# Third FFN: 16 of its 22 hidden units by seven block products in place of eight

## The chip, the cores and the metric

The kernel runs on one core of a Trainium2 chip. The metric is the device time of one execution in microseconds (us). Before the change, three runs took 1701.3, 1697.54 and 1699.22 us: a median of 1699.22. Times below are from these runs or from one profiled execution of the kernel.

## The reference

Two streams of 256 tokens each, 1024 wide in float32 ("latent" and "context"), go through two layers. Each layer has a half-step feed-forward network (FFN), a mixer (attention in the first layer, a gated recurrence in the second), and a second FFN. Scale, shift and gate of each step come from a conditioning vector times a large matrix ("modulation"). The FFN reads:

```python
def half_ffn(h, shift, scale, gate, w_in, w_out, g, b):
    xm = modulate(h, shift, scale)
    a, u = jnp.split(xm @ w_in, 2, axis=-1)
    y = (jax.nn.silu(a) * u) @ w_out
    return post_norm(h, 0.5 * gate * y, g, b)
```

`w_in` is 1024 x 5632 and `w_out` 2816 x 1024. The change concerns the third of the four FFNs, the first of layer 1, which treats both streams (512 tokens).

## The kernel before

**Layout.** Activations lie with the 1024 features in 8 blocks of 128 partitions and the 512 tokens along the free axis: 0 to 255 latent (`LAT`), 256 to 511 context (`CTX`). `xh` and `xl` hold the FFN's modulated input, `h` the residual.

**Precision.** Every float32 operand is split in two parts: ScalarE casts it to a reduced float32 type (`h`, line 194), and VectorE subtracts to get the rest (`l`, line 199, helper `split`). `mm3` (lines 211, 214, 215) makes three matmuls per block: high by high, high by low, low by high. A weight block is 128 x 128.

**One FFN** (`ffn`). The hidden width 2816 is 22 units of 128. `unit_in` for unit j multiplies its `a` and `u` columns (8 blocks each, 3 passes: 48 matmuls) with 512 tokens; `ffn_g` then forms silu(a) * u (lines 521, 522) and splits it into `gh`, `gl`. The units go in two parts of 11. After each part, `unit_out` makes the 8 output blocks: 11 hidden blocks of 3 passes each, accumulated in one PSUM bank, then added to `h` through the gate (line 557). In the first part the four lead units (`LEAD`) run on the latent tokens first and on the context tokens later, as 256-wide matmuls, since the context's norm is still being finished (`LEADSTEP`). In the second part the last four output blocks (`TAIL`) are also made in halves, the latent half first, so that the next norm (`norm`, stepped by `TAILSTEP`) starts while matmuls continue.

**Weights.** A chunk is 128 x 1024 floats (512 KB), loaded by the SyncE queue (`raw`, line 179) into one of `RAW = 3` buffers and split into one of `WB = 7` pairs. A unit needs two chunks, an output block 1.375. `Stream` fetches chunks as they are asked for; `Keep` keeps them for a second use.

**Modulation rows.** `ada` loads one row of the modulation matrix (512 KB, two buffers) and VectorE takes its product with the conditioning vector (line 290). The third FFN carries 32 such rows; `side` spreads them as two after each unit and each output block, in the order written.

**Order of work.** The program is written with tiles. At compile time a planner puts the instructions of each engine in a fixed order: by the order in the program, but an instruction whose inputs or buffers are not ready in the planner's own timing can be overtaken by later ones. Instructions marked with `pin` keep their order among themselves. Tiles of one tag share a fixed number of buffers; here: `raw` 3, `w` 7, `tmp` 6, and 6 PSUM banks for `mm` and 2 for `ps`.

Of the kernel before, what the change touches and what calls it, by code (L numbers as in the profile page):

```python
# [33 lines left out]
SH = 16  # L34
# [2 lines left out]
RMS_EPS = 1e-6  # L37
HEADS = 8
MH = 4
QK_SCALE = 128.0 ** -0.5  # L40
BIG = 1.0e30

RAW = 3
WB = 7

NSTART = 4
# [4 lines left out]
TAIL = 4  # L51
# [90 lines left out]
class Body:  # L142
# [382 lines left out]
    def ffn(self, layer, s, gate, groups, side, start=None):  # L525
        nc, V = self.nc, self.nc.vector
        li = layer * 2 + s
        allg = BOTH
        call = lambda *k: side.get(k, lambda: None)()
        with self.tc.tile_pool(name=f"ffn{li}", bufs=1) as gp:  # L530
            self.gp, self.gt, self.gw, self.gn = gp, {}, T, NFH
            done = 0
            if start:
                start(self)
                done = NSTART

            def unit_in(j, w, g, steps={}):
                n = g[1] - g[0]
                pa, pu = self.mm(), self.mm()
                for k in range(ND):  # L540
                    for part, o in ((0, pa), (1, pu)):
                        self.mm3(o[:, :n], w(k * 2 + part), self.x(k, g), k == 0, k == ND - 1)
                    self.steps(steps.get((j, k), ""))
                self.ffn_g(j, pa, pu, g)

            def unit_out(hf, d, w, g, steps={}):
                t0, t1 = g
                y = self.mm()
                for i in range(NFH):
                    gh, gl = self.gt[hf * NFH + i]  # L550
                    self.mm3(y[:, : t1 - t0], w(d * NFH + i), (gh[:, t0:t1], gl[:, t0:t1]), i == 0, i == NFH - 1)
                    self.steps(steps.get((int(g == CTX), d - (ND - TAIL), i), ""))
                for gg in groups:
                    if gg[0] >= t0 and gg[1] <= t1:
                        v = 0 if gg[0] == 0 else 1
                        z = self.h[:, d, gg[0] : gg[1]]
                        V.scalar_tensor_tensor(z, y[:, gg[0] - t0 : gg[1] - t0], gate()[:, v, d : d + 1], z, ALU.mult, ALU.add)  # L557
                        if hf:
# [4 lines left out]
            for hf in range(2):  # L563
                js = list(range(hf * NFH, (hf + 1) * NFH))[0 if hf else done :]
                if hf == 0 and not start:
                    first = js[:LEAD]
                    ws = {j: Keep(self, [w_in[2 * j + i] for i in range(2)], SH) for j in first}
                    for g in groups:
                        assert len(self.running) == (g == LAT)
                        for j in first:  # L570
                            unit_in(j, ws[j], g, LEADSTEP if g == LAT else {})
                    for j in first:
# [11 lines left out]
                w = Stream(self, [w_out[hf * NFH + i] for i in range(NFH)])  # L584
                body = ND - TAIL if hf else ND
                for d in range(body):
                    unit_out(hf, d, w, allg)
                    call("out", hf, d)
                if body < ND:
                    w = Keep(self, w.chunks, SH, w)  # L590
                    self.fine = True
                    for g in groups:
                        for d in range(body, ND):
                            unit_out(hf, d, w, g, TAILSTEP)
                    self.steps(ENDSTEP)


    def ffn_last(self, layer, gate):
        nc, V, S, a = self.nc, self.nc.vector, self.nc.scalar, self.a
# [662 lines left out]
def emit(ctx, tc, a, out):  # L1262
    b = Body(ctx, tc, a, out)
    nc, V, S = b.nc, b.nc.vector, b.nc.scalar
# [4 lines left out]
    queue = [  # L1269
        [(0, p, both2) for p in range(16, 72)],  # L1270
        [(1, p, both2) for p in range(40)],
        [(1, p, (0,)) for p in range(40, 72)],
    ]
    made = {}

    def once(key, f):
        def get():
            if key not in made:
                made[key] = f()
            return made[key]  # L1280
        return get

    def side(key, coef, keep=(True, True), nxt=True, ada=(), alone=False):
        def pop():
            for _ in range(3 if len(ada) > 40 else 2):
# [6 lines left out]
        s = {}  # L1292
        for j in range(NF):
# [14 lines left out]
    b.ffn(1, 0, once("g2", lambda: b.half_gate(1, 2)), both, side("n3", lambda: b.ln_mod(1, 0, (1, 3)), (True, False), ada=queue[2]))  # L1308
# [9 lines left out]
def _layout(inputs):  # L1318
    f = lambda n: np.asarray(inputs[n])
# [7 lines left out]
    A["ada_w"] = f("ada_w").transpose(0, 2, 1).reshape(2, 72, P, D)  # L1327
    w = f("ffn_w_in").reshape(4, ND, P, 2, NF, P).transpose(0, 4, 2, 1, 3, 5)
    w_in = w.reshape(4, NF, P, 2, 1024).transpose(0, 1, 3, 2, 4).reshape(4, 2 * NF, P, 1024).copy()
    A["ffn_in"] = w_in  # L1330
    A["start_in"] = w[0, :NSTART].transpose(2, 1, 0, 3, 4).reshape(ND, P, 1024)
    w = f("ffn_w_out").reshape(4, 2, NFH, P, ND, P).transpose(0, 1, 4, 2, 3, 5)
    A["ffn_out"] = w.reshape(4, 2 * NFH, 8, P, P).transpose(0, 1, 3, 2, 4).reshape(4, 2 * NFH, P, 1024)
    A["ffn_last"] = f("ffn_w_out")[1, 1].reshape(NF, P, D)
    A["ln_row"] = np.stack([f("ln_g")[1, 2], f("ln_b")[1, 2]]).reshape(2, 4, TL)
# [12 lines left out]
    w = f("att_w_in")[0]  # L1348
# [50 lines left out]
```

## Time and profile before

| | |
|---|---|
| median of three runs | 1699.22 us (1697.54 to 1701.3) |
| span of the profiled execution | 1693.6 us |
| TensorE (PE) busy | 1643.8 us, 97% |
| VectorE (DVE) busy | 1231.7 us, 73% |
| ScalarE (ACT) busy | 656.3 us, 39% |
| GpSimd (POOL) busy | 93.6 us, 6% |
| read from memory | 247.83 MB |

The span runs from the first to the last instruction that the profiler saw; the page gives no other time for that execution, and 1699.22 is 5.6 us more. The page names instructions by engine, line and shape: "128x512 f32 x93 | 54.0, 585" are 93 instructions, 54.0 us busy together, 585 ns each on average. After a second bar stands the engine's idle time before them and what ended it. Matmuls overlap in the pipeline, so a matmul's duration is longer than the distance to the next.

### The profile page before, as it was taken

How to read it: one execution, taken by the hardware profiler on the slowest of the kernel's cores; microseconds unless marked ns; L12 is line 12 of the kernel's file. 1: busy time of each engine (PE TensorE's matmuls, PEld its weight loads, DVE VectorE, ACT ScalarE, POOL GpSimd, SP SyncE). 2: the span in 40 equal slices, each digit the busy share in tenths (PEclk: the TensorE clock that was granted, in tenths of full speed). 3: DMA queues.
4: the chain of work that ended last, by engine and by line, in shares of the span. 5: the costliest groups of instructions: out<-in, count | busy, mean ns of one | idle time of the engine just before them, and what ended most of it. 6: DMA issues, size and time to landing. Idle time of an engine off the chain costs nothing.

```text
span 1693.6 us, 24765 instructions
## 1 busy us (share of the span) xinstructions
PE 1643.8 (97%) x9432; PEld 1441.6 (85%) x9432; DVE 1231.7 (73%) x2681; ACT 656.3 (39%) x1125; POOL 93.6 (6%) x114
## 2 busy tenths in 40 slices
PE   7999999999899999999999999999999999999997
PEld 6888888899887898888888998888889878999986
DVE  6799977659988899996334977643335967998687
ACT  5622133215465452212331543213322645556541
POOL 0000000002321100000000100000001001120000
PEclk9999999999999999999999999999999999999999
DMA  9576765412102346774222257642221232337542
GB/s 356 184 230 231 236 210 199 149 62 77 61 2 82 119 136 234 229 244 152 93 94 75 101 179 247 215 144 98 99 100 63 94 125 76 113 125 246 178 168 94
DMA packets 71910, 250.49 MB, mean 148 GB/s; under 512 B 7920, under 2 KB 10480, under 8 KB 71792
## 3 DMA queue, kind: packets, MB, share of 16 engines
q1 hardware_dynamic: 71072, 248.15, 43.1%
q8 instruction: 74, 1.21, 0.3%
q10 hardware_dynamic: 720, 0.76, 0.1%
q14 instruction: 44, 0.36, 0.1%
HBM read 247.83 MB, written 1.05 MB: 147 GB/s over the span
## 4 chain that ended last, share of the span: by engine, by line
PE 83%; DVE 11%; ACT 3%; DMA 2%; issue 1%; POOL 0%; ACTq 0%; DVEq 0%; SPq 0%
PE t L214 23%; PE t L215 23%; PE t L211 23%; PE t L668 4%; DVE t L199 3%; PE t L1165 2%; PE t L726 2%; PE t L728 2%; PE t L727 2%; ACT t L194 1%; PE t L380 1%; DVE t L473 1%; DVE t L400 1%; DVE t L475 1%; DVE t L1201 1%
## 5 line engine op out<-in xcount | busy, mean ns | idle before, releaser
L211 PE MATMUL t<-t,t 128*128 128x512 f32 (+2 forms) x2540 | 856.1, 339 | 10.1 <-ACT t L194 7.5
L214 PE MATMUL t<-t,t 128*128 128x512 f32 (+2 forms) x2540 | 858.5, 339 | 1.8 <-DVE t L475 1.3
L215 PE MATMUL t<-t,t 128*128 128x512 f32 (+2 forms) x2540 | 854.4, 337 | 1.9 <-DVE t L199 1.9
L199 DVE TENSOR_TENSOR t<-t,t 128x256 fp32r<-128x256 f32 (+2 forms) x793 | 494.8, 659 | 196.4 <-ACT t L194 195.8
L194 ACT CAST t<-t 128x1024 fp32r<-128x1024 f32 (+2 forms) x463 | 397.7, 880 | 587.0 <-PE t L215 311.2
L211 PEld LDWEIGHTS t<-t,t 128*128 128x128 f32 x2540 | 476.6, 188 | 65.7 <-ACT t L194 9.8
L214 PEld LDWEIGHTS t<-t,t 128*128 128x128 f32 x2540 | 477.7, 188 | 56.5 <-DVE t L475 2.5
L215 PEld LDWEIGHTS t<-t,t 128*128 128x128 f32 x2540 | 477.5, 188 | 55.3 <-DVE t L199 2.8
L290 DVE SCALAR_TENSOR_TENSOR t<-t,t 128x1024 bf16<-128x1024 f32 x224 | 262.6, 1220 | 15.9 <-DMA t<-in_ada_w 15.4
L522 DVE TENSOR_TENSOR t<-t,t 128x512 f32<-128x512 f32 (+1 forms) x93 | 54.0, 585 | 112.1 <-PE t L215 92.4
L521 ACT ACTIVATE t<-t 128x512 f32<-128x512 f32 (+1 forms) x93 | 47.4, 515 | 196.9 <-PE t L215 195.0
L417 POOL TENSOR_TENSOR t<-t,t 128x256 f32<-128x256 f32 x30 | 23.3, 777 | 1161.4 <-ACT t L407 1159.9
L557 DVE SCALAR_TENSOR_TENSOR t<-t,t,t 128x256 f32<-128x256 f32 x96 | 42.7, 478 | 54.2 <-PE t L215 54.2
L726 PE MATMUL t<-t,t 128*128 128x256 f32 (+1 forms) x256 | 80.4, 316 | 0.0
L728 PE MATMUL t<-t,t 128*128 128x256 f32 (+1 forms) x256 | 79.7, 314 | 0.0
L727 PE MATMUL t<-t,t 128*128 128x256 f32 (+1 forms) x256 | 79.5, 313 | 0.0
L1165 PE MATMUL t<-t,t 128*128 128x512 f32 (+1 forms) x248 | 54.8, 373 | 11.0 <-ACT t L274 5.2
L1165 PEld LDWEIGHTS t<-t,t 128*128 128x128 f32 x248 | 46.4, 220 | 19.0 <-ACT t L274 5.2
L668 PE MATMUL t<-t,t 128*128 128x512 f32 x264 | 60.0, 389 | 0.0
L668 PEld LDWEIGHTS t<-t,t 128*128 128x128 f32 x264 | 49.5, 188 | 10.2
L407 ACT ACTIVATE t<-t 128x256 f32<-128x256 f32 x72 | 26.1, 413 | 68.3 <-DVE t L400 68.3
L726 PEld LDWEIGHTS t<-t,t 128*128 128x128 f32 x256 | 49.6, 194 | 3.1 <-DVE t L789 0.3
(164 smaller groups left out, 1067.6 us busy)
## 6 DMA issues: line engine op xcount, KB each, us to landing
t<-in_ffn_in SPq DMA_DIRECT2D x168, 512.0 KB, 4.0
t<-in_ada_w SPq DMA_DIRECT2D x139, 512.0 KB, 4.2
t<-in_ffn_out SPq DMA_DIRECT2D x66, 512.0 KB, 3.7
t<-in_ffn_last SPq DMA_DIRECT2D x22, 512.0 KB, 3.7
t<-in_att_in SPq DMA_DIRECT2D x12, 512.0 KB, 3.5
t<-in_att_out SPq DMA_DIRECT2D x8, 512.0 KB, 3.9
t<-in_ml_qk SPq DMA_DIRECT2D x8, 512.0 KB, 3.4
t<-in_ml_v SPq DMA_DIRECT2D x8, 512.0 KB, 4.0
```

The costliest lines, as they stand in the source:

```text
L194: self.behind(self.nc.scalar.copy(h, x))
L199: self.behind(self.nc.vector.tensor_tensor(out=ls, in0=xs, in1=hs.bitcast(F32), op=ALU.subtract))
L211: ins = mm(out, wh, xh, start=first, stop=False)
L214: mm(out, wh, xl, start=False, stop=False)
L215: mm(out, wl, xh, start=False, stop=last)
L290: ins = nc.vector.scalar_tensor_tensor(self.tmp().bitcast(BF16), r, 1.0, self.cb[:, v, :], ALU.mult, ALU.mult, accum_out=to)
L522: V.tensor_tensor(out=sl, in0=sl, in1=pu[:, :n], op=ALU.mult)
L668: pin(nc.tensor.matmul(ys[tt][i], gs[g], ws[k][w][:, i * 512 : (i + 1) * 512], start=k == 0 and g == w == 0, stop=k == NF - 1 and g == 1,))
L726: mm(o, self.xh[:, k, c], wh, start=k == 0, stop=False)
L727: mm(o, self.xh[:, k, c], wl, start=False, stop=False)
L728: mm(o, self.xl[:, k, c], wh, start=False, stop=k == ND - 1)
L1165: mm = lambda *k, **kw: pin(nc.tensor.matmul(*k, **kw))
```

## The change

Units 0 to 5 stay as they were. Units 6 to 21 are computed by Winograd's form of Strassen's method. For one unit, take the 2 x 2 block matrix of weights (rows `a` and `u`; columns the first and the second half of the 1024 features) and the 2 x 2 block matrix of inputs (the feature halves; latent and context tokens). Eight block products give the four results (a and u for each stream); with seven products of sums of blocks the same four results are had. A block product has 4 feature blocks and 256 tokens: 12 matmuls of 256 columns.

- `fold_x` forms the sums of the input blocks once: VectorE adds `xh` and `xl` back, makes four combinations, and splits four results, three into new tiles `th`, `tl` and one over the context half of `xh`, `xl`. It is called twice (two of four feature blocks each), after output blocks 0 and 2 of the first part.
- `fold_w` forms the sums of the weight blocks for each unit, in place in the raw buffers: two chunks give three and a half pairs (two units share one pair for the half).
- `folded` runs the units as generators, each interleaved with the one before it. Several products add into the same PSUM bank, and ScalarE or VectorE reads it between them. The last unit of a part ends between output blocks 0 and 1.
- The parts are 6, 8 and 8 units, so an output block is made in three parts, of 6, 8 and 8 hidden blocks. The last part makes six output blocks in halves (`FOLDTAIL`) in place of four.
- The 32 modulation rows go by a written table: 2 after each lead unit, 3 after units 4 and 5, 4 in the first output part, 14 in the second.
- `RAW` becomes 4, for the whole kernel. The scratch ring of software-generated DMAs is set to 512 bytes (`RING`).

The host's layout of the third FFN's weights follows: in `u`'s chunks of units 6 to 21 the two feature halves are swapped, and the output weights are ordered by the three parts.

```diff
+FOLD = {2: (6, 8, 8)}
+FOLDTAIL = 6
+FOLDPOP = {
+    2: {
+        "lead": (2, 2, 2, 2),
+        "in": {4: 3, 5: 3},
+        "out": {0: (0, 0, 0, 0, 1, 1, 1, 1), 1: (2, 2, 2, 2, 2, 2, 1, 1)},
+    },
+}
+FOLDX = {0: 0, 2: 1}
+RING = 512
...
-RAW = 3
+RAW = 4
...
+FOLDSTEP = {(0, 5, 1): 'bmccccccc', (1, 0, 2): 'c', (1, 0, 6): 'v', (1, 2, 1): 'rxxxxxxxx'}
...
+                folded = None
+                if fold and hf:
+                    self.fine = False
+                    folded = self.folded(js, w_in)
+                    js = []
                 for j in js:
                     unit_in(j, stream(j), allg)
...
-                body = ND - TAIL if hf else ND
-                for d in range(body):
+                body = ND - tail if last else ND
+                begun = 0
+                if folded:
+                    n, begun = parts[hf], 2
+                    ys = [self.mm() for _ in range(2)]
+                    part_out(hf, 0, w, allg, ys[0], range(4))
+                    next(folded)
+                    part_out(hf, 0, w, allg, ys[0], range(4, n - 1))
+                    next(folded, None)
+                    part_out(hf, 1, w, allg, ys[1], range(n - 1))
+                    for d in range(2):
+                        part_out(hf, d, w, allg, ys[d], (n - 1,))
+                        sum_out(hf, d, allg, ys[d])
+                        call("out", hf, d)
+                for d in range(begun, body):
                     unit_out(hf, d, w, allg)
                     call("out", hf, d)
+                    if fold and not hf and d in FOLDX:
+                        self.fold_x(2 * FOLDX[d])
...
+    def fold_x(self, k):
...
+        f11, f12, f21, f22 = whole(k, LAT), whole(k, CTX), whole(ND // 2 + k, LAT), whole(ND // 2 + k, CTX)
+        V.tensor_tensor(out=f11, in0=f11, in1=f12, op=ALU.subtract)
+        V.tensor_tensor(out=f12, in0=f22, in1=f12, op=ALU.subtract)
+        V.tensor_tensor(out=f22, in0=f22, in1=f11, op=ALU.add)
+        V.tensor_tensor(out=f21, in0=f22, in1=f21, op=ALU.subtract)
...
+        self.split(f11, *to[0])
+        h, l = to[1]
+        S.activation(h, f22, AF.Copy, scale=-1.0)
+        V.scalar_tensor_tensor(l, f22, -1.0, h.bitcast(F32), ALU.mult, ALU.subtract)
+        self.split(f12, *to3)
+        self.split(f21, *to[2])
+
+    def fold_w(self, j, w_in):
+
+        V = self.nc.vector
+        r0, r1 = (self.raw(w_in[2 * j + i]) for i in range(2))
+        a = slice(0, 512), slice(512, 1024)
+        ps = [self.pair(sh=SH)]
+        self.split(r0, *ps[0])
...
+        w22 = [x[:, c] for x in p]
+        self.split(r1[:, a[0]], *w22)
+        V.tensor_tensor(out=r1[:, a[0]], in0=r1[:, a[0]], in1=r1[:, a[1]], op=ALU.add)
+        V.tensor_tensor(out=r1[:, a[1]], in0=r1[:, a[1]], in1=r0[:, a[0]], op=ALU.add)
+        V.tensor_tensor(out=r0[:, a[0]], in0=r0[:, a[0]], in1=r1[:, a[0]], op=ALU.add)
+        V.tensor_tensor(out=r0[:, a[1]], in0=r0[:, a[1]], in1=r0[:, a[0]], op=ALU.add)
+        for r in (r0, r1):
+            p = self.pair(sh=SH)
+            self.split(r, *p)
+            ps.append(p)
...
+    def folded(self, js, w_in):
...
+        def product(o, w, x, first):
+            for k in range(half):
+                wh, wl = (y[:, k * P : (k + 1) * P] for y in w)
+                xh, xl = blocks[x](k)
+                for i, (p, q) in enumerate(((wh, xh), (wh, xl), (wl, xh))):
+                    self.pin(nc.tensor.matmul(
+                        o, p, q, start=first and k == i == 0, stop=k == half - 1 and i == 2, skip_group_check=True
+                    ))
+
+        self.open = None
+
+        def begin(j):
+            w = self.fold_w(j, w_in)
+            o0, o1, o2 = (self.mm()[:, :TL] for _ in range(3))
+            sl, u = self.tmp(), self.tmp()
+            product(o0, w["11"], "b11", True)
+            S.copy(sl[:, lat], o0)
+            product(o2, w["12"], "b21", True)
+            yield
+            V.tensor_tensor(out=sl[:, lat], in0=o2, in1=sl[:, lat], op=ALU.add)
+            S.activation(sl[:, lat], sl[:, lat], AF.Silu)
+            product(o0, w["s2"], "t2", False)
+            S.copy(u[:, lat], o0)
+            product(o1, w["s3"], "t3", True)
+            yield
+            product(o0, w["s1"], "t1", False)
+            S.copy(u[:, ctx], o0)
+            V.tensor_tensor(out=u[:, ctx], in0=o1, in1=u[:, ctx], op=ALU.add)
+            yield
+            product(o0, w["s4"], "b22", False)
+            S.activation(sl[:, ctx], o0, AF.Silu)
+            yield
+            product(o1, w["22"], "t4", False)
+            V.tensor_tensor(out=u[:, lat], in0=o1, in1=u[:, lat], op=ALU.add)
...
+            V.scalar_tensor_tensor(sl, u, -1.0, sl, ALU.mult, ALU.mult)
+            self.split(sl, gh, gl)
+
+        before = iter(())
+        for j in js:
+            now = begin(j)
+            next(now)
+            next(before, None)
+            next(now)
+            next(before, None)
+            next(now)
+            before = now
+        return before
...
-    nc = _bacc.Bacc("TRN2", target_bir_lowering=False, num_devices=1)
+    nc = _bacc.Bacc("TRN2", target_bir_lowering=False, num_devices=1, dynamic_dma_scratch_size=RING)
```

More of the change, by code (lines that the diff above doesn't have):

```diff
@@ L562, in ffn @@
             stream = lambda j: Stream(self, [w_in[2 * j + i] for i in range(2)])
-            for hf in range(2):
-                js = list(range(hf * NFH, (hf + 1) * NFH))[0 if hf else done :]
+            for hf in range(len(parts)):
+                last = hf == len(parts) - 1
+                js = list(range(ends[hf] - parts[hf], ends[hf]))[0 if hf else done :]
                 if hf == 0 and not start:
@@ L571, in ffn @@
                             unit_in(j, ws[j], g, LEADSTEP if g == LAT else {})
-                    for j in first:
+                            if fold and g == CTX:
+                                call("in", j)
+                    for j in () if fold else first:
                         call("in", j)
                     js = js[LEAD:]
+                folded = None
[3 more added lines that the diff above has]
+                    js = []
                 for j in js:
@@ L1281, in once, with side, pop @@
         return get
-    def side(key, coef, keep=(True, True), nxt=True, ada=(), alone=False):
-        def pop():
-            for _ in range(3 if len(ada) > 40 else 2):
+    def side(key, coef, keep=(True, True), nxt=True, ada=(), alone=False, fold=None):
+        def pop(n=None):
+            for _ in range(n if n is not None else 3 if len(ada) > 40 else 2):
                 if ada:
@@ L1292, in side @@
         s = {}
+        if fold:
+            for j, n in enumerate(fold["lead"]):
+                s["in", j] = lambda n=n: pop(n)
+            for j, n in fold["in"].items():
+                s["in", j] = lambda n=n: pop(n)
+            for hf, ns in fold["out"].items():
+                for d, n in enumerate(ns):
+                    s["out", hf, d] = lambda n=n: pop(n)
+            return s
         for j in range(NF):
```

73 lines of the change are left out of this document (63 added, 10 removed).

## Prediction

> **What bounds the kernel now.** First the page: shares, queues, the chain that ended last.
>
> ```profile
> span 1693.6 us, 24765 instructions
> PE 1643.8 (97%) x9432; PEld 1441.6 (85%) x9432; DVE 1231.7 (73%) x2681; ACT 656.3 (39%) x1125; POOL 93.6 (6%) x114
> q1 hardware_dynamic: 71072, 248.15, 43.1%
> q8 instruction: 74, 1.21, 0.3%
> q10 hardware_dynamic: 720, 0.76, 0.1%
> q14 instruction: 44, 0.36, 0.1%
> PE 83%; DVE 11%; ACT 3%; DMA 2%; issue 1%; POOL 0%; ACTq 0%; DVEq 0%; SPq 0%
> L211 PE MATMUL t<-t,t 128*128 128x512 f32 (+2 forms) x2540 | 856.1, 339 | 10.1 <-ACT t L194 7.5
> t<-in_ffn_in SPq DMA_DIRECT2D x168, 512.0 KB, 4.0
> t<-in_ffn_out SPq DMA_DIRECT2D x66, 512.0 KB, 3.7
> ```
>
> Matmuls are the chain; the other engines matter where they make matmuls wait. The third FFN lies between 953 and 1310. Next the chain restricted to its middle, 976 to 1290, then windows of PE, which give the pitch (start to start): a window counts each matmul that touches it, so the pitch is (length + one duration) / count; a duration is 0.39 for 512 columns and 0.28 for 256.
>
> ```profile
> by line: PE t L215 33.4%; PE t L214 33.3%; PE t L211 33.3%
> ```
>
> ```profile
> core 0: us, PE busy (x), PEclk, DMA share, GB/s
> 1000.00:1270.00 270.00, 270.00 (x1193) 1.00 0.46 157
> 978.00:996.00 18.00, 18.00 (x162) 1.00 0.43 146
> 1284.00:1296.00 12.00, 12.00 (x104) 1.00 0.13 46
> ```
>
> Nothing but matmuls is on the chain here: PE is never idle and its granted clock is 1.00. So the stage shrinks only by as much as PE gets fewer or cheaper matmuls, provided that all else keeps up. 512 columns cost 270.39 / 1193 = 0.2266 us. 256 columns cost 18.28 / 162 = 0.1128 in the lead units, and 12.28 / 104 = 0.1181 in the output tail, where the same instructions run 5% slower for a reason that the rows do not name. Half of 0.2266 is 0.1133, so narrow matmuls are as efficient as wide ones, or 4% worse.
>
> Last, VectorE and ScalarE, which the change loads. Groups by line and shape for 976 to 1290, VectorE, then ScalarE (busy, mean ns of one):
>
> ```profile
> L199 DVE TENSOR_TENSOR t<-t,t 128x1024 fp32r<-128x1024 f32 x47 | 57.5, 1224 | 65.5 <-ACT t L194 65.4
> L290 DVE SCALAR_TENSOR_TENSOR t<-t,t 128x1024 bf16<-128x1024 f32 x32 | 38.3, 1221 | 7.4 <-DMA t<-in_ada_w 7.3
> L522 DVE TENSOR_TENSOR t<-t,t 128x512 f32<-128x512 f32 x18 | 12.4, 687 | 45.1 <-PE t L215 34.8 <-ACT t L521 10.3
> L199 DVE TENSOR_TENSOR t<-t,t 128x512 fp32r<-128x512 f32 x18 | 12.3, 685 | 0.5 <-ACT t L194 0.5
> L522 DVE TENSOR_TENSOR t<-t,t 128x256 f32<-128x256 f32 x6 | 2.5, 419 | 1.0 <-ACT t L521 1.0
> L557 DVE SCALAR_TENSOR_TENSOR t<-t,t,t 128x256 f32<-128x256 f32 x25 | 11.0, 479 | 19.5 <-PE t L215 19.5
> L194 ACT CAST t<-t 128x1024 fp32r<-128x1024 f32 x60 | 63.2, 1053 | 142.6 <-PE t L215 98.5 <-issue 42.6
> L194 ACT CAST t<-t 128x512 fp32r<-128x512 f32 x18 | 11.1, 616 | 10.5 <-DVE t L522 10.5
> L521 ACT ACTIVATE t<-t 128x256 f32<-128x256 f32 x5 | 1.9, 379 | 4.2 <-PE t L215 4.2
> ```
>
> The duration is not what VectorE pays when its next instruction is ready. Its timeline in the second FFN, in a tail, and in the output part of the third FFN (start, length, count):
>
> ```profile
> 660.17 1.22 DVE L290 SCALAR_TENSOR_TENSOR t<-t,t 128x1024 bf16<-128x1024 f32 x1
> 661.32 0.08 DVE L290 DVE_READ_ACCUMULATOR t<-t,t 128x1 f32 x1
> 661.32 1.23 DVE L290 SCALAR_TENSOR_TENSOR t<-t,t 128x1024 bf16<-128x1024 f32 x1
> ...
> 663.62 0.68 DVE L522 TENSOR_TENSOR t<-t,t 128x512 f32<-128x512 f32 x1
> 664.22 1.82 DVE L199 TENSOR_TENSOR t<-t,t 128x1024 fp32r<-128x1024 f32 x2
> ```
>
> ```profile
> 929.29 1.41 DVE L400 TENSOR_TENSOR t<-t,t 128x256 f32<-128x256 f32 x4 [0.79 <-PE t L380]
> ```
>
> ```profile
> 1089.27 0.88 DVE L557 SCALAR_TENSOR_TENSOR t<-t,t,t 128x256 f32<-128x256 f32 x2 [1.68 <-PE t L215]
> ```
>
> ```profile
> 1085.55 0.17 DVE L342 TENSOR_TENSOR t<-t,t 128x8 f32<-128x8 f32 x1
> 1085.75 0.17 DVE L343 TENSOR_TENSOR t<-t,t 128x8 f32<-128x8 f32 x1
> ```
>
> Starts lie 1.15 apart at 1024 elements of the row product (its accumulator read is covered); the split pair at 664.22 takes 1.82, less 0.685 for its 512-wide half: 1.14. A 512-wide product is 0.60 from its successor; four 256-wide take 1.41, so (1.41 - 0.42) / 3 = 0.33 each; a three-operand 256 is 0.88 - 0.48 = 0.40. Instructions overlap by some 0.08, unless the later one needs the earlier one's result (L343 after L342): then it starts 0.20 later, its length and 0.03.
>
> Two windows with all engines (PE, PEld, DVE, ACT, POOL):
>
> ```profile
> 650.00:700.00 50.00, 50.00 (x222) 41.40 (x221) 49.15 (x80) 15.98 (x21) 0.00 (x0) 1.00 0.72 238
> ```
>
> ```profile
> 976.00:998.00 22.00, 22.00 (x194) 21.84 (x193) 17.33 (x48) 13.49 (x26) 0.00 (x0) 1.00 0.41 139
> ```
>
> The first matters most: VectorE busy 49.15 of 50 us while PE is busy for all 50. The compiled order can keep PE fed by a nearly full VectorE, though much of that work was modulation rows, which no matmul awaits soon.
>
> **The change, part by part.**
>
> *Matmuls.* Units 6 to 21 drop 48 wide matmuls each (768 x 0.2266 = 174.0 us) for 7 products x 4 blocks x 3 passes = 84 narrow ones (1344). At 0.1128 that is 151.6, at 0.1181 it is 158.7: a gain of 22.4 to 15.3. The products add twelve times running into one bank, like the tail, but read the tokens' tiles, like the lead; I take the middle, 0.116: 155.9, a gain of 18.1 (9.74 per unit, from 10.88).
>
> *Weights.* Before, a unit cost VectorE two splits and ScalarE two casts. Now three 1024 splits (3 x 1.14), one 512 split (0.60), four 512 sums (2.40, plus about 0.24 where one sum waits for the one before: 0.69 + 0.03 instead of 0.60, twice): 6.7 us. Then three 256 sums from PSUM (1.0), a three-operand 512 (0.66: 0.60 + the 0.06 that three operands add at 256), and the 512 split (0.60): 8.9 per unit, against 9.74 on PE, 92%. ScalarE: 3 x 1.05 + 0.62 + five 256 readouts at 0.38 + 0.62 = 6.3. Neither is the bound if pitches hold. By durations, 3 x 1.224 + 0.685 + 4 x 0.687 + 3 x 0.419 + 0.75 + 0.685 = 9.8, with the two signals 9.9, and VectorE would set the pace (first rival).
>
> *How far ahead.* Seven weight pairs serve 3.5 per unit, four raw buffers two per unit, six PSUM banks three per unit: a unit can be prepared while its predecessor is multiplied. Before, casts already run until pairs are full; they wait for a matmul to release one:
>
> ```profile
> ACT t L194 <- PE t L215: 98.5, 26, 4.4
> ```
>
> Queued behind such a cast on ScalarE are now readouts of the shared bank, which PE needs two products later (24 x 0.116 = 2.8 us); behind a running cast a readout comes after at most 1.05 + 0.38. For PE's waits I scale the page's L211 row: 7.5 us behind casts over the 168 + 66 FFN chunks, 0.03 each; four casts in 16 units give 2 us. Bounds: 0 (the 650 row) and, with VectorE at its durations, 16 x (9.9 - 9.74) = 2.6 more.
>
> *Entry to the first folded part.* PE: 22.0 for the context lead, 2 x 10.88 for units 4 and 5, 8 x 18 x 0.2266 = 32.6 of output: 76.4. VectorE: 17.3 as in the row at 976, 18 rows (8 + 6 + 4) x 1.15 = 20.7, two gate products and splits 2.4, six output chunks in quarters 24 x 0.33 = 7.9, 16 sums x 0.40 = 6.4, token combinations 2 x (8 x 0.60 + 0.66 + 3 x 0.60) = 14.5: 69.2. With the first unit's 6.7 it is 75.9: it just fits. I take 1.5 us of stall; bounds 0 and, by durations (10% more, 83.5), 7. ScalarE's part of the combinations, 8 x 0.6, has room.
>
> *Second output part.* VectorE: 8 chunks x 1.14 + 6.4 + 14 rows x 1.15 = 31.6 in 8 x 24 x 0.2266 = 43.5: room for the next unit's 6.7. The sums of a third part (6.4) vanish there. Without this cover the second entry would cost up to 6.7 as well. Moving rows changes neither their 32 issues on SP nor their buffers; what is queued behind them there are weight loads, at 1 MB per 9.7 us far below the 157 GB/s of the wide window.
>
> *Tail.* Six blocks of 24 in halves for four of 33: 24 more narrow matmuls for 12 wide, 24 x 0.118 - 12 x 0.2266 = +0.1.
>
> *Fourth raw buffer, everywhere; smaller ring.* Loads wait for splits:
>
> ```profile
> SPq L179 <- DVE t L199: 1105.5, 289, 84.6
> ```
>
> A fourth buffer lets each issue one chunk earlier, but in this stage no matmul waits for a load. Elsewhere the longest load on the chain after the start is this:
>
> ```profile
> 540.03 4.93 DMA t<-in_att_out
> ```
>
> ```profile
> 953.70 0.70 PE L380 MATMUL t<-t,t 128*128 128x256 f32 x2 [1.20 <-DVE t L357]
> ```
>
> So at best -4.9. At worst the re-planned order of other stages costs PE two more idle stretches like the 1.20 at the norm here, +2.4. I take 0, since the work that hides the loads stays. The page lists no software-generated queue among its four, so the ring is 0.
>
> *Sum:* -18.1 + 2 + 1.5 + 0.1 = -14.5. Against the span: 1693.6 - 14.5 = 1679.1; with every bound on one side, -22.4 - 4.9 = -27.3 and -15.3 + 2 + 2.6 + 7 + 2.4 = -1.3. The median of the runs, 1699.2, is 5.6 above this span, which I take for launch and end and keep: 1684.7.
>
> **Rivals.**
>
> *VectorE becomes the bound (same or slightly faster).* With no overlap a unit takes 9.9 and the entry is 7 late: 16 x (10.88 - 9.9) - 7 - 2 of casts = a gain of 6.7: 1692.5. For it: chained sums and cross-engine waits leave less overlap than independent rows. Against it: 49.15 in 50 with PE full. [...]
>
> *Preparation does not run ahead (slower).* Each engine's order is fixed at compile time. Suppose VectorE gets the sums of unit j+1 behind the last readout of unit j, since they sit behind it in one queue and pairs come free late. From the end of product s1: cast 1.05 and difference 1.14 give 2.2; half split 2.8; sums 5.4; cast and difference of s2 7.6; s2, s3, the old unit's 22, s1 follow at 1.39 each: 13.2 per unit, 16 x 2.3 = +37: 1736. It decides from 10.88 per unit, that is once PE waits 1.14 us in each. For it: the pairs and PSUM are exactly two units deep. Against it: the casts' 98.5 us above are waits of work that had already run ahead.
>
> *No gain from narrow matmuls.* At 10.88 / 84 = 0.1295 us per matmul the time stays 1699. Only the 0.1181 row leans that way.
>
> *More than forecast.* 0.1128, no stall, and the attention's load hidden: -22.4 - 4.9: 1672.
>
> **Chances.** Forecast 0.58 (own range 1679 to 1691), VectorE bound 0.20, no run-ahead 0.17, no gain 0.02, more 0.03. About 0.2% (3.4 us) can be told from no change. Faster: 0.57 + 0.03 + 0.12 of the VectorE case = 0.72; same: 0.01 + 0.07 + 0.01 = 0.09; slower: 0.17 + 0.01 + 0.01 = 0.19. The range, 1676 to 1702, leaves out most of the third case and of the last.
>
> **What would show it.** Right: windows of the folded parts with PE full, 256-wide pitch 0.113 to 0.118, unit period near 9.8, VectorE 90 to 95% there; at most one idle stretch of PE, behind L199 or a sum, at the first folded unit. VectorE bound: VectorE above 98% in the folded windows, matmuls idle behind VectorE in every unit. No run-ahead: PE idle over 1 us in each unit behind a cast or VectorE, while VectorE is idle behind matmuls. The forecast is wrong if unit periods exceed 10.3, or if other stages move by over 3 us.

## The result, and the profile after

The changed kernel takes 1684.28 us, the median of five runs (1683.0 to 1685.22), and the kernel before 1697.65 (five runs, 1696.43 to 1701.3): a ratio of 0.9916, interval 0.9904 to 0.9928, or 13.4 us less. The prediction was 1684.7. It came out right, but two of its terms were off by some 3 and 5 us, in opposite directions. Of all executions reported below, one of a repeat (the kernel with rows in the tail, further down) took 3316.84 us, twice the others, for a reason that the record does not show; it is left out of that ratio.

The page of the changed kernel: span, busy time, the chain that ended last, and the group of the new products (L717). L224 is now what L211 was.

```profile
span 1683.3 us, 26222 instructions
PE 1631.4 (97%) x10020; PEld 1457.7 (87%) x10020; DVE 1333.7 (79%) x2880; ACT 700.4 (42%) x1230; POOL 93.7 (6%) x114
PE 73%; DVE 18%; DMA 3%; ACT 3%; issue 2%; POOL 0%; ACTq 0%; DVEq 0%; SPq 0%; POOLq 0%
L717 PE MATMUL t<-t,t 128*128 128x256 f32 x1344 | 161.4, 282 | 5.6 <-ACT t L207 2.5
```

PE is busy for 12.4 us less and VectorE for 102 us more; the chain still runs mostly over PE, but VectorE's share of it grew from 11% to 18%.

How long is the stage itself? I take it from its first 512-wide matmul to the first matmul pair of the norm behind it, in the timelines of PE, before and after:

```profile
997.92 0.40 PE L211 MATMUL t<-t,t 128*128 128x512 f32 x1
...
1321.58 0.70 PE L380 MATMUL t<-t,t 128*128 128x256 f32 x2 [1.10 <-DVE t L357]
```

```profile
996.72 0.40 PE L224 MATMUL t<-t,t 128*128 128x512 f32 x1
...
1312.22 0.70 PE L393 MATMUL t<-t,t 128*128 128x256 f32 x2 [0.61 <-DVE t L370]
```

That is 323.66 us before and 315.50 after: 8.2 less, where 14.5 were forecast. (A second profile of the same changed kernel gave 313.6, so 8.2 to 10.1.) The spans of these two profiles differ by 10.3 us, so in them 2.1 lie outside the stage; the medians of the runs differ by another 3.1.

Where the stage lost what it should have gained is seen in windows over the two folded parts, PE, PEld, VectorE, ScalarE, GpSimd, then PE's granted clock: each part whole, then its steady middle.

```profile
1051.00:1134.60 83.60, 79.38 (x650) 78.20 (x649) 72.52 (x104) 45.85 (x77) 0.00 (x0) 0.96 0.42 136
1060.00:1130.00 70.00, 68.79 (x574) 68.14 (x574) 60.16 (x87) 40.33 (x68) 0.00 (x0) 0.97 0.36 120
1181.00:1257.80 76.80, 75.44 (x649) 74.56 (x649) 68.33 (x111) 42.08 (x75) 0.00 (x0) 1.00 0.39 127
1190.00:1250.00 60.00, 59.91 (x523) 59.54 (x522) 52.66 (x79) 33.39 (x61) 0.00 (x0) 1.00 0.32 102
```

The same number of matmuls takes 83.6 us in the first folded part and 76.8 in the second, and the first has a granted clock of 0.96. VectorE is busy for 86 and 88% of the steady windows, so it is not the bound. PE's timeline and windows at the entry to the first part show the loss:

```profile
1053.50 0.63 PE L717 MATMUL t<-t,t 128*128 128x256 f32 x4
1056.63 0.76 PE L717 MATMUL t<-t,t 128*128 128x256 f32 x2 [2.50 <-ACT t L207]
1057.89 6.79 PE L717 MATMUL t<-t,t 128*128 128x256 f32 x34 [0.50 <-DVE t L212]
```

```profile
1053.90:1057.90 4.00, 1.00 (x5) 0.85 0.57 174
1057.90:1063.20 5.30, 5.30 (x25) 0.50 0.57 200
1075.00:1094.00 19.00, 19.00 (x164) 1.00 0.35 112
1100.00:1114.00 14.00, 14.00 (x126) 1.00 0.29 102
```

PE waits 2.50 us for a cast and 0.50 for a split, with two matmuls between, and then 25 matmuls run at half clock (0.50). From the last matmul ahead of the wait, which starts at 1053.85, to the first back at full pace, at 1063.57, 29 matmuls take 9.7 us instead of 3.3: 6.4 lost, some 4.0 by waiting and 2.4 by the half clock. What PE waited for, on VectorE and ScalarE:

```profile
1052.46 1.22 DVE L303 SCALAR_TENSOR_TENSOR t<-t,t 128x1024 bf16<-128x1024 f32 x1 [0.24 <-DMA t<-in_ada_w]
1053.61 0.69 DVE L690 TENSOR_TENSOR t<-t,t 128x512 f32<-128x512 f32 x1
1054.22 0.68 DVE L688 TENSOR_TENSOR t<-t 128x512 f32<-128x512 f32 x1
1054.82 0.68 DVE L691 TENSOR_TENSOR t<-t 128x512 f32<-128x512 f32 x1
```

```profile
1055.54 2.00 ACT L207 CAST t<-t 128x1024 fp32r<-128x1024 f32 x2 [2.41 <-DVE t L691]
```

The last two weight sums of the first folded unit (L690 and L691; the L688 between them is the next unit's first sum) stand in VectorE's order behind the four modulation rows of the first output part (L303), of which the last is shown. They come out at 1055.5; the cast behind them starts at once, and PE gets its third product 2.5 us late.

The pace of the narrow matmuls has two values: by the last two PE windows above, (19.00 + 0.28) / 164 = 0.1176 us and (14.00 + 0.28) / 126 = 0.1133. Over all folded matmuls at full clock, 756 started less than 0.116 us before their successor and 540 between 0.116 and 0.126, on average 0.1152; they are called 113 and 118 ns below. The 1344 need 154.9 us at that. They took 83.5 + 76.8 and 4 x 1.41 for the products placed between output blocks, 165.9: so 11.0 us were lost, 6.4 of them at the first entry.

### The profile page after: what moved, and what is told of

Read it like the earlier page. It is cut to its first block, busy times and chain, and to the rows that moved or that the text cites. A ratio compares the mean times of both kernels' runs of the same rounds, so it can differ in the third digit from the quotient of the medians.

```text
span 1683.3 us, 26222 instructions
## 1 busy us (share of the span) xinstructions
PE 1631.4 (97%) x10020; PEld 1457.7 (87%) x10020; DVE 1333.7 (79%) x2880; ACT 700.4 (42%) x1230; POOL 93.7 (6%) x114
## 4 chain that ended last, share of the span: by engine, by line
PE 73%; DVE 18%; DMA 3%; ACT 3%; issue 2%; POOL 0%; ACTq 0%; DVEq 0%; SPq 0%; POOLq 0%
PE t L224 19%; PE t L228 19%; PE t L227 19%; DVE t L212 5%; PE t L717 4%; PE t L831 4%; PE t L1328 2%; ACT t L207 2%; DMA t<-in_ada_w 2%; PE t L889 1%; PE t L891 1%; PE t L890 1%; PE t L393 1%; DVE t L486 1%; DVE t L488 1%
## 5 line engine op out<-in xcount | busy, mean ns | idle before, releaser
L224 PE MATMUL t<-t,t 128*128 128x512 f32 (+2 forms) x2288 | 759.6, 334 | 10.1 <-ACT t L207 6.7
L227 PE MATMUL t<-t,t 128*128 128x256 f32 (+2 forms) x2288 | 760.4, 333 | 1.5 <-DVE t L488 1.2
L228 PE MATMUL t<-t,t 128*128 128x256 f32 (+2 forms) x2288 | 757.2, 332 | 2.7 <-DVE t L212 2.7
L207 ACT CAST t<-t 128x1024 fp32r<-128x1024 f32 (+2 forms) x501 | 426.4, 873 | 539.5 <-PE t L228 237.6
L212 DVE TENSOR_TENSOR t<-t,t 128x256 fp32r<-128x256 f32 (+3 forms) x846 | 527.7, 660 | 134.5 <-ACT t L207 134.0
L224 PEld LDWEIGHTS t<-t,t 128*128 128x128 f32 x2288 | 429.9, 189 | 55.5 <-ACT t L207 9.2
L227 PEld LDWEIGHTS t<-t,t 128*128 128x128 f32 x2288 | 432.1, 189 | 45.5 <-DVE t L488 2.0
L228 PEld LDWEIGHTS t<-t,t 128*128 128x128 f32 x2288 | 430.9, 189 | 46.0 <-DVE t L212 3.6
L303 DVE SCALAR_TENSOR_TENSOR t<-t,t 128x1024 bf16<-128x1024 f32 x224 | 262.8, 1219 | 13.3 <-DMA t<-in_ada_w 13.1
L717 PE MATMUL t<-t,t 128*128 128x256 f32 x1344 | 161.4, 282 | 5.6 <-ACT t L207 2.5
L717 PEld LDWEIGHTS t<-t,t 128*128 128x128 f32 x1344 | 159.3, 191 | 8.0 <-ACT t L207 2.7
L535 DVE TENSOR_TENSOR t<-t,t 128x512 f32<-128x512 f32 (+1 forms) x77 | 42.9, 562 | 71.6 <-PE t L228 60.6
L534 ACT ACTIVATE t<-t 128x512 f32<-128x512 f32 (+1 forms) x77 | 37.9, 499 | 148.0 <-PE t L228 147.1
L582 DVE SCALAR_TENSOR_TENSOR t<-t,t,t 128x256 f32<-128x256 f32 x112 | 50.1, 478 | 40.3 <-PE t L228 40.1
L889 PE MATMUL t<-t,t 128*128 128x256 f32 (+1 forms) x256 | 79.2, 311 | 0.0
L891 PE MATMUL t<-t,t 128*128 128x256 f32 (+1 forms) x256 | 78.6, 309 | 0.0
L890 PE MATMUL t<-t,t 128*128 128x256 f32 (+1 forms) x256 | 78.4, 308 | 0.0
L1328 PEld LDWEIGHTS t<-t,t 128*128 128x128 f32 x248 | 46.8, 222 | 18.9 <-ACT t L287 5.0
L831 PEld LDWEIGHTS t<-t,t 128*128 128x128 f32 x264 | 49.5, 188 | 10.2
```

The lines of the kernel that those rows point to most:

```text
L207: self.behind(self.nc.scalar.copy(h, x))
L212: self.behind(self.nc.vector.tensor_tensor(out=ls, in0=xs, in1=hs.bitcast(F32), op=ALU.subtract))
L224: ins = mm(out, wh, xh, start=first, stop=False)
L227: mm(out, wh, xl, start=False, stop=False)
L228: mm(out, wl, xh, start=False, stop=last)
L303: ins = nc.vector.scalar_tensor_tensor(self.tmp().bitcast(BF16), r, 1.0, self.cb[:, v, :], ALU.mult, ALU.mult, accum_out=to)
```

## The experiments

All ratios are to the kernel before, run on the same chip.

### What else the change contains: the fourth raw buffer, the three parts

The kernel before with a fourth raw buffer and the small ring alone:

```diff
-RAW = 3
+RAW = 4
...
-    nc = _bacc.Bacc("TRN2", target_bir_lowering=False, num_devices=1)
+    nc = _bacc.Bacc("TRN2", target_bir_lowering=False, num_devices=1, dynamic_dma_scratch_size=512)
```

> The kernel before with four raw buffers and the small scratch ring, and nothing else of the change. The changed kernel's profile shows 7.7 us less in the third FFN and some 2.6 us less outside it. Theory A (the fourth buffer, or the re-planned order that comes with it, gives the part outside): 2 to 5 us faster than before, with the third FFN as long as before. Theory B (the part outside is spread between executions): within 1.5 us of before, and the fold alone gives the 13 us.

And the changed kernel without the fold: 6, 8 and 8 units, the row table, the tail of six and the fourth buffer stay, all units have eight block products.

```diff
-                if fold and hf:
-                    self.fine = False
-                    folded = self.folded(js, w_in)
-                    js = []
...
-                    if fold and not hf and d in FOLDX:
-                        self.fold_x(2 * FOLDX[d])
```

> The changed kernel with all 22 units by the eight plain block products: three parts of 6, 8 and 8 units, tail of six blocks, the table of modulation rows, four raw buffers stay; no combinations of tokens or weights. Theory A: as raw4_only within 1.5 us, since the third part and the longer tail are hidden, so that the fold itself is worth the distance to the changed kernel, 8 to 10 us. Theory B: within 1.5 us of the kernel before, the fold worth 13 us. A third way: the three parts or the new table of rows cost or gain something themselves; then it lies over 2 us from raw4_only.

The first gave 1695.05 us against 1698.38, 0.9984 (0.9975 to 0.9994); the second 1695.78, 0.9985 (0.9976 to 0.9995). So the fourth buffer and the small ring, which were not run apart, are together worth some 3 us (1.0 to 4.2 by the interval), and the three parts, the tail and the row table cost nothing on top that these runs can tell. The stage says the same: 323.66 us in the first, and 323.55 in the second (998.93 to 1322.48).

From unfolded to changed, the ratios differ by 0.0069, 11.7 us; the stage by 8.0 to 10. The gain of the fourth buffer lies outside the stage, but its place is not found. One candidate is the place where the prediction had looked: the load of the attention's output weights in the chain of waits. From the three chains, before, with four raw buffers alone and after, the last matmuls ahead of the load and the load:

```profile
535.16 0.45 PE t L840 x4
...
540.03 4.93 DMA t<-in_att_out
```

```profile
534.12 0.45 PE t L840 x4
...
539.00 4.65 DMA t<-in_att_out
```

```profile
534.10 0.45 PE t L1003 x4
...
538.97 4.18 DMA t<-in_att_out
```

The first matmul behind the load starts at 546.62, 545.26 and 544.75, so 1.4 and 1.9 us earlier. But the load follows the matmuls ahead of it by 4.87 to 4.88 us in all three: PE was 1.0 us ahead already, and the rest is the length of the load itself. Nor does the lead last: the third FFN's first 512-wide matmul starts at 997.92 before and at 997.64 in the raw-buffer kernel, 0.3 us earlier. One profile does not resolve the rest: between executions of one kernel the time outside the stage varies by up to 4 us (1367.8 and 1367.5 in two profiles of the changed kernel, 1366.7 and 1370.7 in two of a later one).

### Do the four rows cause the first stall? Three other places for them

Four modulation rows of the first output part go to the second:

```diff
-        "out": {0: (0, 0, 0, 0, 1, 1, 1, 1), 1: (2, 2, 2, 2, 2, 2, 1, 1)},
+        "out": {0: (0, 0, 0, 0, 0, 0, 0, 0), 1: (3, 3, 2, 2, 2, 2, 2, 2)},
```

> The changed kernel with the four modulation rows of the first output part moved to the second (18 rows there). In the changed kernel TensorE stands idle for 2.8 + 0.8 us at the first folded unit and then has 25 narrow matmuls at 213 ns, half the clock, 2.4 us more. Theory A (VectorE is late there by the rows in front of the first unit's sums, 4 x 1.15 = 4.6 us): both go, 5 to 6 us faster than the changed kernel, at the price of up to 2 us at the second entry, where VectorE has 38 us of work for 39. Theory B (the first unit waits for a buffer or for ScalarE's casts): the idle stretch stays above 2.5 us and the time within 1 us of the changed kernel.

It takes 1689.69 us, 0.9948 (0.9934 to 0.9961): 5 us slower than the changed kernel where the theory had it faster. The first half of the theory held: the stall at the first entry is gone, and the part takes 77.5 us instead of 83.5. But a larger one appears at the second entry. PE's timeline there, PE's window behind it, ScalarE's timeline and VectorE's:

```profile
1190.32 0.79 PE L717 MATMUL t<-t,t 128*128 128x256 f32 x2 [9.35 <-ACT t L728]
```

```profile
1190.50:1195.30 4.80, 4.80 (x23) 0.50 0.27 100
```

```profile
1189.79 0.21 ACT L207 CAST t<-t 128x16 fp32r<-128x16 f32 x1 [7.70 <-DVE t L404]
1189.90 0.36 ACT L728 COPY t<-t 128x256 f32<-128x256 f32 x1
```

```profile
1188.16 1.22 DVE L303 SCALAR_TENSOR_TENSOR t<-t,t 128x1024 bf16<-128x1024 f32 x1 [1.25 <-DMA t<-in_ada_w]
...
1189.50 0.25 DVE L404 COPY t<-t 128x8 f32<-128x8 f32 x2
```

PE waits 9.35 us for the readout of a product's bank (L728). ScalarE had nothing else to do; but in its fixed order a tiny cast (128 x 16) of a later norm's coefficients stands ahead of that readout, and it waits 7.70 us for a copy (L404) that needs modulation rows up to the one at 1188.16, which itself waited 1.25 us for its load. Matmuls thus wait for rows that no matmul of this stage needs.

The four rows one each after folded units 7 to 10:

```diff
-        "in": {4: 3, 5: 3},
-        "out": {0: (0, 0, 0, 0, 1, 1, 1, 1), 1: (2, 2, 2, 2, 2, 2, 1, 1)},
+        "in": {4: 3, 5: 3, 7: 1, 8: 1, 9: 1, 10: 1},
+        "out": {0: (0, 0, 0, 0, 0, 0, 0, 0), 1: (2, 2, 2, 2, 2, 2, 1, 1)},
...
             next(now)
+            call("in", j)
             before = now
```

> The changed kernel with the same four rows placed after the folded units 7 to 10, one each: VectorE's load per such unit rises from some 8.4 to 9.6 us, with 9.5 to 9.9 of matmuls. Theory A (VectorE has 12% to spare in the folded units): the entry stall goes as in rows_later and the folded units stay at their pace, 5 to 6 us faster than the changed kernel. Theory B (VectorE is nearly the bound there): each of the four units gets 0.5 to 1.2 us longer, and the gain is 2 to 4 us at most.

1685.21 us, 0.9923 (0.9909 to 0.9937): the same as the changed kernel. Again the first entry is free, and again a stall takes its place, at 1094, with 22 matmuls at half clock (0.50) behind it. PE's wait there, and VectorE's timeline:

```profile
PE t L717 <- ACT t L207: 2.4, 1, 2.4
```

```profile
1093.49 1.21 DVE L303 SCALAR_TENSOR_TENSOR t<-t,t 128x1024 bf16<-128x1024 f32 x1
...
1094.63 0.68 DVE L212 TENSOR_TENSOR t<-t,t 128x512 fp32r<-128x512 f32 x1
1095.23 0.68 DVE L691 TENSOR_TENSOR t<-t 128x512 f32<-128x512 f32 x1
...
1097.02 3.69 DVE L212 TENSOR_TENSOR t<-t,t 128x1024 fp32r<-128x1024 f32 x3 [0.78 <-ACT t L207]
```

The chain of waits runs over the moved row (L303), the half-wide split, the last sum (L691), the cast and its split to PE. So a row stands ahead of the sum once more. (An earlier cast, at 1087.94, had waited 1.6 us for a weight load; what that adds is not shown.) By this chain, what decides is what stands ahead of the sums in VectorE's order, not VectorE's total.

Next, some of the 18 rows of the output parts go to the first two blocks of the last part, which had none, and the first part has none:

```diff
-        "out": {0: (0, 0, 0, 0, 1, 1, 1, 1), 1: (2, 2, 2, 2, 2, 2, 1, 1)},
+        "out": {0: (0, 0, 0, 0, 0, 0, 0, 0), 1: (2, 2, 2, 2, 2, 1, 1, 0), 2: (3, 3)},
```

> The changed kernel with the four modulation rows of the first output part and two of the second moved behind output blocks 0 and 1 of the third part (three each); 12 stay in the second. Where the rows were moved before, the first entry's idle stretch vanished and one of 9.6 us (second entry) or 2.7 us (inside a unit) came. Theory A (VectorE owes the rows at each entry, and has room only after the last folded unit: 3.5 of 6.2 us busy there and 30.6 of 39.4 in the tail): no stretch over 1 us at either entry, no half clock, tail as long as before within 1 us, 5 to 8 us faster than the changed kernel. Theory B (the row loads, which share the load queue with the weights, upset whatever stands next to them): a new stretch of 2 us or more in the tail or the norm behind it, and no net gain.

1680.35 us, 0.9891 (0.9876 to 0.9905). To compare it closely, it ran a second time beside the unchanged changed kernel, on one chip:

> The changed kernel once more, unaltered, beside rows_tail_again on one chip, since the interval of rows_tail (0.9876 to 0.9905) and that of the changed kernel (0.9904 to 0.9928) touch. Expected: 0.990 to 0.993 of the kernel before; the idle stretch and the half clock at the first folded unit as in its first profile.

> The kernel of rows_tail once more, unaltered. Theory A (the entry stall is worth its 6 us, less some 2.5 us because its folded matmuls run at 118 rather than 113 ns): 3 to 5 us faster than after_again on the same chip. Rival: the first distance came from the chip or the hour; within 1.5 us.

1685.27 us, 0.9916 (0.9903 to 0.9929), for the changed kernel, and 0.9881 (0.9866 to 0.9896) for this one, from three executions of 1677.78 to 1679.98 us: by the ratios 5.9 us less, more than the 3 to 5 expected. It beats both kernels. Its two folded parts, in windows of the second run:

```profile
1052.99:1130.30 77.31, 76.47 (x649) 75.95 (x648) 68.23 (x96) 44.36 (x77) 0.00 (x0) 1.00 0.38 128
1176.70:1253.00 76.30, 76.30 (x649) 76.26 (x649) 65.23 (x104) 43.89 (x75) 0.00 (x0) 1.00 0.40 127
```

No half clock, hardly any idle time, and a stage of 309.7 us in both profiles: 14.0 less than before, which is nearly what the prediction gave to the stage (14.5).

### How much of the stall is the half clock?

28 narrow matmuls that nobody reads are put between the second and the third product of the first folded unit, so that PE works while it would wait:

```diff
             product(o2, w["12"], "b21", True)
+            if j == FOLD[2][0]:
+                fill = self.ps()[:, :TL]
+                for i in range(28):
+                    self.pin(nc.tensor.matmul(fill, w["11"][0][:, :P], blocks["b11"](0)[0], start=i == 0, stop=i == 27, skip_group_check=True))
             yield
```

> The changed kernel with 28 more narrow matmuls, whose result nobody reads, between products 12 and s2 of the first folded unit, where TensorE is idle for 3.6 us. Theory A (the 25 matmuls at 213 ns follow from the idle stretch): the clock stays whole, the products s2, s3 and s1 of that unit take 1.4 us each in place of 2.6 to 3.6, and the time falls by 2 to 2.5 us although nothing is ready earlier. Theory B (those matmuls are slow because of what VectorE, ScalarE or loads do then): they stay at 213 ns, and the time stays or rises by up to 1 us.

1685.14 us, 0.9927 (0.9915 to 0.9939). PE's timeline and windows at the entry:

```profile
1056.42 3.46 PE L733 MATMUL t<-t,t 128*128 128x256 f32 x28
1059.72 0.40 PE L717 MATMUL t<-t,t 128*128 128x256 f32 x2
```

```profile
1056.00:1060.00 4.00, 4.00 (x35) 1.00 0.67 214
1060.50:1066.00 5.50, 5.50 (x48) 1.00 0.56 192
```

The clock stays at 1.00 and the products behind run at full pace: the 48 from 1060.48 take 5.73 us together, which puts them (5.73 - 0.28) / 47 = 0.116 us apart. So here the idle time does cause the half clock, and the first part is 2.1 us shorter (81.4). The whole kernel is no faster, against the expectation. In the profiled execution 1105 folded matmuls ran at 118 ns and only 231 at 113, which by the two paces costs about as much as the clock gained: (1105 - 540) x 0.0043 = 2.4 us. What changed the pace is not shown.

### What sets the pace of 113 or 118 ns?

The weight pairs of the folded units lie 16 elements into their buffers (`SH`). With 48 instead:

```diff
-        ps = [self.pair(sh=SH)]
+        ps = [self.pair(sh=SHM)]
...
-            p, self.open = self.pair(sh=SH), 1
+            p, self.open = self.pair(sh=SHM), 1
...
-            p = self.pair(sh=SH)
+            p = self.pair(sh=SHM)
```

> The changed kernel with the folded weight pairs 48 instead of 16 elements into their buffer. In the changed kernel 530 of the folded matmuls came at 118 ns and 760 at 113, in long runs of the one or the other that begin at waits. Theory A (the pace is set by how weight load and matmul fall into step at a wait, not by addresses): both paces still there, mean pitch 114 to 117 ns, time within 1.5 us of the changed kernel. Theory B (addresses of weights against tokens set it): one pace alone, 118 (2 to 3 us slower) or 113 (2 us faster).

The same edit on the kernel with rows in the tail, with `sh=0`:

> rows_tail with the folded weight pairs at offset 0 of their buffer instead of 16 elements. At 48 all folded matmuls ran at 118 ns, at 16 both paces came. Theory B of sh48 (the place of weights against tokens decides whether 113 can be reached): another mix than at 16, either all 118 (up to 1.5 us slower than rows_tail) or mostly 113 (up to 4 us faster). Theory A (only the step at waits): a mix as in rows_tail, 300 of 1330 at 113, within 1 us.

and with `sh=32`:

> rows_tail with the folded weight pairs at offset 32. Same question as offset 0: by theory B another mix of 113 and 118 ns than at 16 (all 118: up to 1.5 us slower than rows_tail; mostly 113: up to 4 us faster); by theory A a mix as in rows_tail, within 1 us.

They take 1686.75 (0.9937, 0.9925 to 0.9949), 1681.89 (0.9901, 0.9887 to 0.9914) and 1681.99 (0.9898, 0.9885 to 0.9912). None is better than 16. A steady PE window of each, in the order 48, 0, 32:

```profile
1200.00:1240.00 40.00, 40.00 (x342) 1.00 0.32 106
```

```profile
1200.00:1240.00 40.00, 40.00 (x335) 1.00 0.35 105
```

```profile
1200.00:1240.00 40.00, 40.00 (x336) 1.00 0.34 106
```

That is (40.00 + 0.28) / 342 = 0.1178, 0.1202 and 0.1199 us. At 48 nearly all matmuls run at 118 ns, at 0 and 32 at about 120, a pace that was not expected. At 16 the shares differ from profile to profile: in the second profile of the changed kernel 1133 ran at 113 and 159 at 118, in the first 756 and 540, and in the repeat of the kernel with rows in the tail, also at 16, 123 and 1215. So the place of the weights has a part in it at 0 and 32, the change to 48 cannot be told from what 16 itself shows, and what switches the same kernel between 113 and 118 is not settled. If all ran at 113, it would be worth up to 1344 x (0.1176 - 0.1133) = 5.8 us, an estimate from the two windows of the changed kernel.

### When does preparation stop running ahead?

The changed kernel with three raw buffers:

```diff
-RAW = 4
+RAW = 3
```

> The changed kernel with three raw buffers instead of four. A folded unit holds two for the whole of its preparation, so the next unit can have only one of its two loads early. Theory A (the fourth buffer is what lets preparation run ahead): stretches of 0.5 us or more in most folded units, 5 to 15 us slower than the changed kernel. Theory B (preparation is ahead anyway by the pairs): folded units as fast as now, and only the 2.7 us that four buffers gave without the fold are lost.

1699.48 us, 1.0014 (1.0003 to 1.0025): the whole gain is gone. A window of the first folded part, and the waits in the whole part:

```profile
1100.00:1124.00 24.00, 21.07 (x178) 20.27 (x178) 18.85 (x29) 11.57 (x20) 0.00 (x0) 1.00 0.28 93
```

```profile
DVE t L212 <- ACT t L207: 19.3, 15, 3.3
ACT t L207 <- DVE t L691: 15.4, 8, 3.3
PE t L717 <- ACT t L207: 7.1, 8, 2.3
PE t L717 <- DVE t L212: 6.1, 8, 0.8
```

PE is idle for 2.9 of 24 us, in each unit twice for about 0.7 us; over the part it waits 7.1 us behind casts and 6.1 behind splits, while VectorE waits for ScalarE and ScalarE for VectorE. The first folded part takes 93.1 us, the stage 329.4 (999.61 to 1328.97), 13.9 to 15.7 more than with four buffers.

## Why the prediction was right, point by point

*What bounds the stage.* Right: matmuls, and the others only where they make matmuls wait. The units behind the first take on average 9.7 us in the second part (9.74 forecast) and 10.1 in the first.

*Matmuls, 18.1 less.* Right within its bounds: 154.9 us instead of 155.9, 19.1 less. The 0.116 was the middle of two measured paces, and both paces occur.

*Weights.* Right: VectorE 8.9 us per unit forecast; 60.16 of 70 us at 10.1 per unit is 8.7, and 52.66 of 60 at 9.7 is 8.5. The starts overlap as in the rows before: the sums at 1053.61, 1054.22 and 1054.82 lie 0.61 and 0.60 apart with durations of 0.69 and 0.68. The 90 to 95% expected of VectorE were 86 and 88%. ScalarE's 6.3 were 5.8 and 5.4.

*Waits behind casts, +2.* About right: of the 11.0 us lost, 2.8 lie outside the two entries. The mechanism is the one forecast, a readout on ScalarE (L734) behind a running cast; here, in the first part, PE and then ScalarE:

```profile
1123.61 1.09 PE L717 MATMUL t<-t,t 128*128 128x256 f32 x7 [0.75 <-ACT t L734]
```

```profile
1122.24 1.05 ACT L207 CAST t<-t 128x1024 fp32r<-128x1024 f32 x1 [0.90 <-DVE t L691]
1123.19 0.37 ACT L734 COPY t<-t 128x256 f32<-128x256 f32 x1
```

The sign "at most one idle stretch of PE" did not hold: besides two at each entry there are four such gaps, 0.36 to 1.03 us from start to start.

*First entry, +1.5.* The step that failed: 6.4 us, inside its bounds of 0 to 7. "It just fits" added up VectorE's work over 76.4 us and compared totals; when it came to the moment, four rows stood ahead of the two sums that PE's next product needed. The other part of the size was not in the prediction at all: behind the idle time 25 matmuls at half clock, at 0.213 us instead of 0.115, cost 2.4.

*Second output part, 0.* Some 1.8 us instead, at the second entry: two gaps of 1.13 and 0.69 us from start to start, each with one slow matmul behind it (0.22 us, at a granted clock of 1.00). The room on VectorE was there; PE waited for readouts on ScalarE, the same kind of wait that grew to 9.35 us where rows were moved there. The first of them stood behind two casts that had waited for a sum on VectorE (L691).

*Tail, +0.1.* Right: from the first half to the norm 40.55 us against 38.03 before plus 12 wide matmuls, 2.7: -0.2.

*Fourth raw buffer, 0.* Mis-sized: with the small ring some 3 us less by the runs, inside its bounds (-4.9 to +2.4). The load that it looked at is not shown to be the source: it was issued no sooner behind the matmuls ahead of it, and of the 1.4 us there 0.3 were left where the stage begins. Where the gain arises stays open.

*The 5.6 us around the span.* Wrong in its cause. In every execution the device time is 1.8 to 2.1 us above the span (1685.22 and 1683.3 in the run profiled here). Later runs of the kernel before had spans from 1692.0 to 1700.3; the one profiled, 1693.6, was a short one. To hang the difference on the median of the runs was right all the same, as it is the median that is compared; but with two more runs that median fell from 1699.22 to 1697.65, so that 1684.7 lies within 0.5 us of 1684.28 is luck as well.

*The sum.* The stage gave 8.2 to 10.1 us instead of 14.5, the rest of the kernel some 3 instead of 0. The two errors partly cancel, and 13.4 in total against 14.5 looks better than the working was. The kernel with the rows in the tail, where the entries are free, shows that the stage's 14.5 were there to be had: 14.0.

*The rivals.* VectorE as the bound: refuted, with 86 and 88% and PE full for 59.91 of 60 us. Preparation that doesn't run ahead: not the case here, but real. With three raw buffers the ratio is 1.0014 instead of 0.9916, 16.6 us more, of which 13.9 to 15.7 lie in the stage. The prediction looked for this rival in the weight pairs and in PSUM; with both unchanged, the raw buffers alone decide it. (The sums are formed in the raw buffers, so a unit holds both of its buffers until the last split: that is read from the code, not measured by itself.) The prediction had counted four raw buffers among what lets a unit be prepared ahead, but asked what the fourth is worth only outside the stage, where it put 0; inside, it was the condition of the gain. No gain from narrow matmuls: refuted, 0.1152 against the 0.1295 it needed. More than forecast: not here, since the entry stalled.

## What to carry to other kernels

When a stage is made shorter by moving work to another engine, total busy time says only whether it fits; the place to price is the entry, where the first result of the new work is needed, and there the order on each queue counts: ask what stands ahead of it, and what that itself waits for. Work that nobody needs soon (here modulation rows) belongs where nothing that is needed soon is queued behind it: rows of the output parts went with a loss of 6.4 us in one place, a stall of 9.35 us and half clock (0.50) behind it in another, and with neither in a third. A lead seen at one place of the chain is a gain only if it is still there further on: here 1.4 us at a load had become 0.3 at the stage, so compare the start of the same matmul at several places.

## What the runs showed of the hardware

The half clock was not expected. About 3 us of idle time within 4 us, with two matmuls between, was followed by 5.3 us at a granted clock of 0.50; in two other kernels 9.35 us and 2.42 + 0.47 us of idle time were followed by 23 and 22 matmuls at 0.50, and with matmuls that nobody reads in the gap the clock stayed at 1.00. The longest single gap ahead of the half clock in the changed kernel was 2.50 us.

Nor were the two paces of one and the same narrow matmul, 113 and 118 ns at a granted clock of 1.00, about 120 with the weights at other places; the cause of the switch stays open.
